# A matrix product on one core: first tiles of x on two DMA queues, and the last 256 columns of w loaded as fp32

## The chip, the cores and the metric

The kernel runs on one core of a Trainium2 chip. The metric is device microseconds of one execution. The core has a matrix engine (TensorE, PE in the profile), two engines that copy, cast and add (VectorE or DVE, ScalarE or ACT), GpSimd (POOL), and SyncE (SP), which here issues DMAs only. ScalarE and GpSimd can issue DMAs too, each on a queue of its own; all queues feed the same 16 DMA engines.

## The reference

```python
def setup_inputs():
    batch, seq, hidden = 16, 512, 768
    return {"x": randn(batch, seq, hidden) as float32,
            "w_qkv": randn(hidden, 3 * hidden) as float32}

def reference(x, w_qkv):
    qkv = np.matmul(x, w_qkv)
    q, k, v = the three blocks of 768 columns of qkv
    return np.stack([q, k, v], axis=0).astype(np.float32)
```

So x is a matrix of 8192 rows and 768 columns, w has 768 rows and 2304 columns, and the three blocks of 768 columns of the product go to three planes of the output.

## The kernel before

**Tiles.** x is worked in 32 pairs of row tiles; a pair `p` holds 256 rows, its row tile `r` 128. The 2304 columns of w are cut into two blocks of 1024 (`q` = 0, 1, each of two slices of `CB` = 512 columns) and the 256 columns between them, the remainder (`REM`, tile `w_rem`). The inner dimension of 768 is six slices `j` of 128; `KH` = 3 of them are a K half `h`. From the third pair on, a pair against a block is not multiplied in eight products of halves but in seven, on sums and differences of quarters of x (`sums_x`, tile `s`) and of w (`sum_w`, tiles `t1` to `t4` and `b22`): `do(u, n)` emits product `n` of a `Quad` `u`, with its evacuation from PSUM. Products 1 and 2 use bf16 copies (`xb` and `b1`), the others 32-bit operands. The remainder is multiplied plainly in bf16.

**The start.** The first two pairs (`ND` = 2) are multiplied plainly in bf16, slice by slice, as w lands. All of this order is written out by hand (`manual_schedule`): every engine runs its instructions in the order in which they are emitted, and waits on semaphores for what they need.

- `load_row` loads a row tile of x as 128 rows of 3 KB, `cast_row` casts it to bf16 (VectorE one half of the columns, ScalarE the other, by `copy_halves`), `turn_row` turns it with six transposes on TensorE (L190) into two PSUM tiles and returns a function that copies them to `xb` (again one half each). All four row tiles go on SyncE's queue, one after the other.
- `touch` are two small DMAs on ScalarE's queue, 128 pieces of 128 bytes each: of w, and of x's third row tile. Nothing reads their result.
- `load_slices` puts the slices of the first 1024 columns of w on SyncE's queue behind x: for the first 512 columns slice 0 in two halves, then slices 1 to 5; then six slices of the second 512.
- `busy(n)` are dummy matmuls of zeros (L458). Between the row tiles' turns stand `busy(8)`, `busy(2)`, `busy(2)`, `busy(1)`.
- `block(0, 0, ...)` multiplies the first two pairs (four row tiles) by the first 512 columns of w (L487), when all four row tiles are turned. For slice 0 it does three row tiles on the first 256 columns, the three on the other 256, and then the fourth; after that four whole matmuls per slice. `cast_j` casts a slice of w for it. `block(0, 1, ...)` follows with the second 512 columns; its last three slices are done row tile by row tile.
- `w_rem` is loaded by two DMAs of GpSimd that cast to bf16 on the way (L450). `hold` keeps GpSimd back until the last slice of the first 512 columns has landed.
- `rems_by_halves` then multiplies the two pairs by the remainder: 24 matmuls of 256 columns (L334), all of K half 0, then all of K half 1.
- Meanwhile VectorE turns the third pair of x (`transpose`, L154), ScalarE rounds its rows to bf16 (`round_row`, L207), VectorE makes `t1` to `t4` (`sum_w`, L120) and the sums of x, and GpSimd casts `b22` (L556). Then `u = quad(2, 0)`, the third pair against the first block, starts with `do(u, 1)` and `do(u, 2)`. VectorE's addition in `do(u, 2)` (L273) comes after `t3` and the sums of x.

A DMA is issued on SyncE only when the DMA eight places before it has landed. PSUM has eight banks, which all products and turns share. The tag `"o"` has five buffers of 8 KB per partition, for the quads' outputs.

After the start, `two`, `group` and `last` run the other pairs in a regular order; the change does not touch them.

Of the kernel before, what the change touches and what calls it, by code (L numbers as in the profile page):

```python
# [10 lines left out]
def kernel(  # L11
# [20 lines left out]
    nc = tc.nc  # L32
    P = 128
    G = 32
    B, T, H = x.shape
    M = B * T
    K = H
    N3 = w_qkv.shape[1]
    KT = K // P
# [72 lines left out]
    def sum_w(q, n):  # L112
        t1, t2, t3, t4 = ts[q]
        o, in0, in1 = {
            1: (t1, stage[q, 0, 1], stage[q, 0, 0]),
            2: (t2, stage[q, 1, 1], t1),
            3: (t3, stage[q, 1, 1], stage[q, 0, 1]),
            4: (t4, stage[q, 1, 0], t2),
        }[n]
        nc.vector.tensor_tensor(o, in0, in1, op=sub)  # L120
# [10 lines left out]
    def load_x_rows(p, parts=range(8)):  # L131
        if p not in xin:
            xin[p] = xin_pool.tile([P, 2 * P // G, KC], fp32, name="xin")
        rows = x_flat[p * 2 * P:(p + 1) * 2 * P, :].rearrange("(g b) k -> b g k", b=G)
        for n in parts:
            r, i = divmod(n, 4)
            gs = slice(r * P // G, (r + 1) * P // G)
            nc.sync.dma_start(
                xin[p][i * G:(i + 1) * G, gs], rows[:, gs, i * KC:(i + 1) * KC]
            )  # L140
# [21 lines left out]

    def load_row(p, r):
        if r == 0:
            xin[p] = xin_pool.tile([P, 2, K], fp32, name="xin")
        row = (2 * p + r) * P
        nc.sync.dma_start(xin[p][:, r], x_flat[row:row + P, :])

    def copy_halves(dst, src):
        nc.vector.tensor_copy(out=dst[0], in_=src[0])
# [4 lines left out]
    def cast_row(p, r):  # L177
        if r == 0:
            xc[p] = s_pool.tile([P, 2, K], bf16, name="xc", tag="s")
        halves = (slice(0, K // 2), slice(K // 2, K))  # L180
        copy_halves([xc[p][:, r, n] for n in halves], [xin[p][:, r, n] for n in halves])

    def turn_row(p, r):
        if r == 0:
            xb[p] = xb_pool.tile([P, KT, 2 * P], bf16, name="xb", tag="xb")
        cols = xc[p][:, r, :].rearrange("m (p j) -> m j p", j=KT)
        ks = (slice(0, KH), slice(KH, KT))
        ps = [ps_pool.tile([P, KH, P], bf16, name="ps") for _ in ks]
        for j in range(KT):
            nc.tensor.transpose(ps[j // KH][:, j % KH, :], cols[:, j, :], eye)  # L190
        return lambda: copy_halves(
            [xb[p][:, n, r * P:(r + 1) * P] for n in ks], [t[:] for t in ps]
        )
# [8 lines left out]
    def round_row(p, r, eng):  # L202
        n = slice(r * P, (r + 1) * P)
        if r == 0:
            xb[p] = xb_pool.tile([P, KT, 2 * P], bf16, name="xb", tag="xb")
        if eng is act:
            eng.activation(xb[p][:, :, n], xf[p][:, :, n], ident)  # L207
        else:
            eng.tensor_copy(out=xb[p][:, :, n], in_=xf[p][:, :, n])
# [46 lines left out]
    def bank():  # L256
        return ps_pool.tile([P, CB], fp32, name="ps")
# [61 lines left out]
    def rem_copied(p, ps, eng=nc.sync):  # L319

        def copied():
            o = or_pool.tile([P, 2, REM], fp32, name="orem")
            act.activation(o[:], ps[:], ident)  # L323
            return lambda: eng.dma_start(rows_of(1, p, R_OFF - H, R_OFF - H + REM), o[:])

        return copied

    def rems_by_halves(pairs):
        banks = [ps_pool.tile([P, 2, REM], fp32, name="ps") for _ in pairs]
        for h in range(2):  # L330
            for p, ps in zip(pairs, banks):
                for r in range(2):
                    for j in range(KH):
                        nc.tensor.matmul(  # L334
                            ps[:, r, :], xb[p][:, h * KH + j, r * P:(r + 1) * P],
                            w_rem[h][:, j, :], start=(h == 0 and r == 0 and j == 0),
                            stop=(h == 1 and j == KH - 1), skip_group_check=True,
                        )
        return [rem_copied(p, ps) for p, ps in zip(pairs, banks)]

    def two(a, b, early, u=None, turns=()):

# [83 lines left out]
    ND = 2  # L426
    zero = xb_pool.tile([P, CB], bf16, name="zero", tag="xb")
    nc.vector.memset(zero[:], 0.0)
    load_row(0, 0)
    touch = m_pool.tile([P, 2, G], fp32, name="touch")  # L430
    nc.scalar.dma_start(touch[:, 0], w_qkv.rearrange("(p j) n -> p j n", j=KT)[:, 0, :G])  # L431
    nc.scalar.dma_start(touch[:, 1], x_flat[2 * P:3 * P, :G])
    nc.scalar.activation(tiny[:], zero[:, :1], ident)
    make_identity(nc, eye)
    load_row(0, 1)
    load_row(1, 0)
    load_row(1, 1)
    half = CB // 2
    load_slices(0, [(0, 1, 0, half), (0, 1, half, CB)] + [(j, 1, 0, CB) for j in range(1, KT)])
    load_slices(1, [(j, 1, 0, CB) for j in range(KT)])  # L440
    load_x_rows(2)

    def hold(src):
        mark = m_pool.tile([P, 1], fp32, name="mark")
        nc.gpsimd.tensor_copy(out=mark[:], in_=src)

    hold(stage[0, 1, 0][:, KH - 1, :1])
    for h in range(2):
        rows = w_qkv.rearrange("(p j) n -> p j n", j=KT)[:, h * KH:(h + 1) * KH]
        nc.gpsimd.dma_start(w_rem[h][:], rows[:, :, R_OFF:R_OFF + REM])  # L450
    hold(xin[2][:, 0, :1])
    load_blocks(1, 0)

    def busy(n):

        ps = bank()
        for _ in range(n):
            nc.tensor.matmul(ps[:], zero[:, :P], zero[:], start=True, stop=True)  # L458

    def cast_j(q, c, w, j, eng=act, n=slice(0, CB)):  # L460
        src = stage[q, j // KH, c][:, j % KH, n]
        if eng is act:
            eng.activation(w[:, j, n], src, ident)  # L463
        else:
            eng.tensor_copy(out=w[:, j, n], in_=src)
# [59 lines left out]

    busy(8)
    cast_row(0, 0)
    turned = [turn_row(0, 0)]
    busy(2)
    turned[0]()  # L530
    cast_row(0, 1)
    turned.append(turn_row(0, 1))
    busy(2)
    cast_row(1, 0)
    turned[1]()
    turned.append(turn_row(1, 0))
    busy(1)
    cast_row(1, 1)
    turned[2]()
    cast_j(0, 0, b1[0], 0, dve, lo)  # L540
    turned.append(turn_row(1, 1))
    cast_j(0, 0, b1[0], 0, dve, hi)
    turned[3]()
    for j in range(1, KT):
        cast_j(0, 0, b1[0], j, dve)
    late0 = block(0, 0, b1[0], first)
    for j in range(KH):
        cast_j(0, 1, bt, j, dve)
    for f in late0:
# [3 lines left out]
    cast_j(0, 1, bt, 4, act)  # L553
    cast_j(0, 1, bt, 5, act)
    sum_w(0, 2)
    nc.gpsimd.tensor_copy(out=b22[0][:], in_=stage[0, 1, 1])  # L556
    late = block(
        0, 1, bt, [((j, ), range(4)) for j in range(KH)] + [(range(KH, KT), range(4))]
    )
    rems = rems_by_halves(range(2))  # L560
    transpose(2, 2)

    late[0]()
    late[1]()
    round_row(2, 0, act)
    rem_stores = [rems[0]()]
    late[2]()
    late[3]()
    round_row(2, 1, act)
    rem_stores.append(rems[1]())  # L570
    load_blocks(1, 1)
    for store in rem_stores:
        store()
    load_x_rows(3)
    for p in range(2):
        store_quad(quads[p, 0])
# [2 lines left out]
    sums[0](nc.gpsimd)  # L579
    sums[1](dve)  # L580
    sums[2](dve)
    sum_w(0, 3)
    sums[3](dve)
    sums[4](dve)

    u = quad(2, 0)
    do(u, 1)
    do(u, 2)
    cast_j(1, 0, b1[1], 0)
    rem2 = rem(2)  # L590
    middle(u, (5, 6))
# [120 lines left out]
```

## Time and profile before

| | |
|---|---|
| median of 3 runs | 359.97 us (359.88 to 360.47) |
| the profiled execution | 360.26 us, its span 358.5 us |
| TensorE busy | 351.8 us, 98% of the span |
| VectorE, ScalarE, GpSimd busy | 65%, 52%, 50% |
| HBM read and written | 32.28 MB and 75.50 MB, 301 GB/s over the span |

The page lists for each engine how long it was busy. The chain of waits follows the work that ended last back to the start, at each step to what released it. The timeline lists instructions in order of time with the idle time before them and what ended it. Where the duration of matmuls is given for a group, the matmuls overlap: their starts stand closer than one lasts. In the windows each engine's busy time in a stretch is followed by the granted clock, the busy share of the DMA engines and the GB/s they moved.

### The profile page before, as it was taken

To read this page: it belongs to the slowest core of one execution; us is meant where nothing else is said; L and a number is where in the kernel's file an instruction comes from. 1 tells how busy PE (TensorE), PEld (TensorE's weight loads), DVE (VectorE), ACT (ScalarE), POOL (GpSimd) and SP (SyncE) were. 2 spreads that over 40 slices of the span, in tenths; PEclk is the share of its full clock that TensorE was granted. 3 is DMA by queue.
4 is the path that set the end of the run, shared out by engine and by line. 5 is a ranking of instruction groups with operands and counts; after the bars stand their busy time and mean duration, and the time that the engine had idled before them with its cause. 6 is when DMAs were issued, how large, how long until landed. Compare 5 with 4: busy or idle time off the path is not lost.

```text
span 358.5 us, 5212 instructions
## 1 busy us (share of the span) xinstructions
PE 351.8 (98%) x1760; PEld 252.6 (70%) x1780; DVE 231.7 (65%) x245; ACT 185.5 (52%) x316; POOL 178.5 (50%) x187
## 2 busy tenths in 40 slices
PE   8999999999999999999999999999999999999995
PEld 4465577767768687786867768687776867768764
DVE  3789776878475675746676474676647577544643
ACT  5469644445545545454554545545454544545443
POOL 0223775582664717447372664717447371754420
PEclk9999999999999999999999999999999999999999
DMA  7998999999999898989989799898989989755767
GB/s 265 347 373 313 323 353 360 369 346 342 339 298 317 286 261 328 261 317 299 289 323 250 309 283 332 282 264 329 268 293 307 294 321 251 312 217 224 273 243 256
DMA packets 82106, 107.73 MB, mean 301 GB/s; under 512 B 5408, under 2 KB 62240, under 8 KB 82080
## 3 DMA queue, kind: packets, MB, share of 16 engines
q1 hardware_dynamic: 74288, 101.86, 86.1%
q10 hardware_dynamic: 6992, 5.15, 5.9%
q0 software_dynamic: 800, 0.39, 0.8%
q8 instruction: 14, 0.23, 0.3%
q14 instruction: 12, 0.10, 0.1%
HBM read 32.28 MB, written 75.50 MB: 301 GB/s over the span
## 4 chain that ended last, share of the span: by engine, by line
PE 93%; DMA 4%; ACT 1%; ACTq 1%; issue 0%
PE ps L251 78%; PE ps L306 11%; PE ps L487 4%; DMA st<-in_w_qkv_dram 3%; DMA touch<-in_x_dram 1%; PE ps L334 1%; ACT o L286 0%; ACTq L385 0%; ACT orem L399 0%; ACT both L463 0%; ACTq L431 0%; ACTq L401 0%; ACTq L399 0%
## 5 line engine op out<-in xcount | busy, mean ns | idle before, releaser
L251 PE MATMUL ps<-t,s 128*128 128x512 f32 x720 | 178.5, 396 | 0.0
L251 PEld LDWEIGHTS ps<-t,s 128*128 128x128 f32 x720 | 134.9, 188 | 29.8 <-ACT o L276 0.3
L154 DVE STREAM_TRANSPOSE xf<-xin 128x1536 f32<-128x1536 f32 (+1 forms) x33 | 91.2, 2767 | 2.5 <-DMA xin<-in_x_dram 2.5
L218 POOL TENSOR_TENSOR s<-xf 128x384 fp32r<-128x384 f32 x29 | 30.8, 1061 | 116.4 <-PE ps L251 115.0
L251 PE MATMUL ps<-b,xb 128*128 128x512 bf16 x342 | 81.7, 379 | 1.2
L283 DVE TENSOR_TENSOR o<-o,ps 128x512 f32<-128x512 f32 x58 | 39.7, 685 | 60.2 <-ACT o L282 60.2
L251 PEld LDWEIGHTS <-xb 128*128 128x128 bf16 x360 | 33.8, 98 | 36.9 <-issue 4.7
L273 DVE TENSOR_TENSOR o<-o,ps 128x512 f32<-128x512 f32 x60 | 39.0, 681 | 29.5 <-PE ps L251 22.4
L282 ACT ACTIVATE o<-ps 128x512 f32<-128x512 f32 x58 | 34.7, 598 | 44.2 <-PE ps L251 44.2
L276 ACT ACTIVATE o<-ps 128x512 f32<-128x512 f32 x60 | 36.0, 600 | 36.6 <-PE ps L251 34.0
L289 DVE TENSOR_TENSOR o<-o,ps 128x512 f32<-128x512 f32 x60 | 41.1, 687 | 20.7 <-PE ps L251 19.6
L260 ACT ACTIVATE o<-ps 128x512 f32<-128x512 f32 x60 | 35.7, 597 | 31.3 <-PE ps L251 18.3
L251 PE MATMUL ps<-b,s 128*128 128x512 f32 x180 | 50.4, 389 | 0.0
L198 POOL CAST xb<-xf 128x1536 bf16<-128x1536 f32 x28 | 41.0, 1464 | 16.7 <-DVE xf L154 16.7
L286 ACT ACTIVATE o<-ps 128x512 f32<-128x512 f32 x60 | 35.9, 598 | 24.3 <-PE ps L251 21.3
L306 PE MATMUL ps<-w_rem,xb 128*128 128x256 bf16 x360 | 44.6, 273 | 0.0
L306 PEld LDWEIGHTS <-xb 128*128 128x128 bf16 x360 | 34.9, 98 | 11.0 <-issue 1.1
L251 PEld LDWEIGHTS ps<-b,s 128*128 128x128 f32 x180 | 33.8, 188 | 7.1
L219 POOL TENSOR_TENSOR s<-s,xf 128x384 fp32r<-128x384 f32 x29 | 29.3, 1009 | 1.3
L220 POOL TENSOR_TENSOR s<-xf 128x384 fp32r<-128x384 f32 x29 | 29.3, 1009 | 0.0
L222 POOL TENSOR_TENSOR s<-xf,s 128x384 fp32r<-128x384 f32 x29 | 29.3, 1009 | 0.0
L323 ACT ACTIVATE orem<-ps 128x512 f32<-128x512 f32 x31 | 18.5, 597 | 20.7 <-PE ps L306 10.9
(47 smaller groups left out, 127.4 us busy)
## 6 DMA issues: line engine op xcount, KB each, us to landing
out_dram<-o SPq DMA_DIRECT2D x62, 768.0 KB, 4.5
xin<-in_x_dram SPq DMA_DIRECT2D x90, 192.0 KB, 6.5
out_dram<-o SPq DMA_DIRECT2D x65, 256.0 KB, 3.7
out_dram<-orem SPq DMA_DIRECT2D x31, 256.0 KB, 5.5
xin<-in_x_dram ACTq DMA_DIRECT2D x22, 192.0 KB, 6.9
st<-in_w_qkv_dram SPq DMA_DIRECT2D x11, 256.0 KB, 5.2
st<-in_w_qkv_dram SPq DMA_DIRECT2D x3, 768.0 KB, 10.0
xin<-in_x_dram SPq DMA_DIRECT2D x4, 384.0 KB, 4.5
```

The lines of the kernel that those rows point to most:

```text
L154: lambda g=g: nc.vector.transpose(turned[:, g:g + n], rows[:, g:g + n])
L198: nc.gpsimd.tensor_copy(out=xb[p][:], in_=t[:])
L218: 1: lambda g: g.tensor_tensor(s[:, 1], a21, a22, op=add),
L251: nc.tensor.matmul(ps[:], lhs[j], rhs[j], start=(start and j == 0), stop=(j == KH - 1), skip_group_check=True,)
L260: nc.scalar.activation(u.o[:, 0, :CB], u.x[:], ident)
L273: nc.vector.tensor_tensor(c11, c11, u.z[:], op=add)
L276: nc.scalar.activation(c12, u.x[:], ident)
L282: nc.scalar.activation(c22, u.x[:], ident)
L283: nc.vector.tensor_tensor(c22, c22, u.y[:], op=add)
L286: nc.scalar.activation(c21, u.x[:], ident)
L289: nc.vector.tensor_tensor(c12, c12, u.y[:], op=add)
L306: nc.tensor.matmul(ps, xb[p][:, j, r * P:(r + 1) * P], w_rem[j // KH][:, j % KH, :], start=(j == 0), stop=(j == KT - 1), skip_group_check= ...
```

## The change

The second row pair goes on ScalarE's queue, beside the first on SyncE's, and the `touch` of x is dropped. VectorE casts 448 of the 768 columns of a row tile instead of 384, and copies four of the six turned slices instead of three. The first three row tiles are turned, and their first 256 columns multiplied, before the fourth row tile is turned (`turn_last`, called inside `block`); slice 0's second 256 columns are cast by ScalarE. The remainder's columns of w come as fp32 by SyncE's queue in two K halves, each in front of one half of the third pair's load; GpSimd casts them to bf16, ahead of `b22`. They use a buffer of the tag `"o"`. `hold` and GpSimd's DMAs are gone. Products 1 and 2 of `u` stand between the two K halves of the remainder's products (`rems_half`), the remainders are evacuated behind `u`'s product 1 and the rounding of the third pair's second row tile, and VectorE's addition of product 2 comes ahead of `t3`.

```diff
-    def load_row(p, r):
+    def load_row(p, r, eng=nc.sync):
...
-        nc.sync.dma_start(xin[p][:, r], x_flat[row:row + P, :])
+        eng.dma_start(xin[p][:, r], x_flat[row:row + P, :])
...
     def cast_row(p, r):
...
-        halves = (slice(0, K // 2), slice(K // 2, K))
+        halves = (slice(0, K * 7 // 12), slice(K * 7 // 12, K))
...
     def turn_row(p, r):
...
-        ks = (slice(0, KH), slice(KH, KT))
-        ps = [ps_pool.tile([P, KH, P], bf16, name="ps") for _ in ks]
-        for j in range(KT):
-            nc.tensor.transpose(ps[j // KH][:, j % KH, :], cols[:, j, :], eye)
+        ks = (slice(0, KT - 2), slice(KT - 2, KT))
+        ps = [ps_pool.tile([P, n.stop - n.start, P], bf16, name="ps") for n in ks]
+        for n, t in zip(ks, ps):
+            for j in range(n.start, n.stop):
+                nc.tensor.transpose(t[:, j - n.start, :], cols[:, j, :], eye)
...
-    def rems_by_halves(pairs):
-        banks = [ps_pool.tile([P, 2, REM], fp32, name="ps") for _ in pairs]
-        for h in range(2):
...
-        return [rem_copied(p, ps) for p, ps in zip(pairs, banks)]
+    def rems_half(pairs, banks, h):
+        for p, ps in zip(pairs, banks):
+            for r in range(2):
+                for j in range(KH):
+                    nc.tensor.matmul(
+                        ps[:, r, :], xb[p][:, h * KH + j, r * P:(r + 1) * P],
+                        w_rem[h][:, j, :], start=(h == 0 and r == 0 and j == 0),
+                        stop=(h == 1 and j == KH - 1), skip_group_check=True,
+                    )
...
-    load_row(0, 0)
-    touch = m_pool.tile([P, 2, G], fp32, name="touch")
-    nc.scalar.dma_start(touch[:, 0], w_qkv.rearrange("(p j) n -> p j n", j=KT)[:, 0, :G])
-    nc.scalar.dma_start(touch[:, 1], x_flat[2 * P:3 * P, :G])
+    touch = m_pool.tile([P, G], fp32, name="touch")
+    nc.scalar.dma_start(touch[:], w_qkv.rearrange("(p j) n -> p j n", j=KT)[:, 0, :G])
+    for r in range(2):
+        load_row(0, r)
+        load_row(1, r, nc.scalar)
...
-    load_row(0, 1)
-    load_row(1, 0)
-    load_row(1, 1)
...
-    load_x_rows(2)
-
-    def hold(src):
-        mark = m_pool.tile([P, 1], fp32, name="mark")
-        nc.gpsimd.tensor_copy(out=mark[:], in_=src)
-
-    hold(stage[0, 1, 0][:, KH - 1, :1])
-    for h in range(2):
-        rows = w_qkv.rearrange("(p j) n -> p j n", j=KT)[:, h * KH:(h + 1) * KH]
-        nc.gpsimd.dma_start(w_rem[h][:], rows[:, :, R_OFF:R_OFF + REM])
-    hold(xin[2][:, 0, :1])
+    st_rem = o_pool.tile([P, KT, REM], fp32, name="str", tag="o")
+    load_w(st_rem[:, :KH], 0, KH, R_OFF, REM)
+    load_x_rows(2, range(4))
+    load_w(st_rem[:, KH:], KH, KH, R_OFF, REM)
+    load_x_rows(2, range(4, 8))
     load_blocks(1, 0)
...
     busy(8)
     cast_row(0, 0)
-    turned = [turn_row(0, 0)]
-    busy(2)
-    turned[0]()
+    turned = turn_row(0, 0)
+    busy(3)
+    turned()
     cast_row(0, 1)
-    turned.append(turn_row(0, 1))
-    busy(2)
     cast_row(1, 0)
-    turned[1]()
-    turned.append(turn_row(1, 0))
-    busy(1)
+    turned = [turn_row(0, 1), turn_row(1, 0)]
+    busy(3)
+    for f in turned:
+        f()
+    cast_j(0, 0, b1[0], 0, dve, lo)
     cast_row(1, 1)
-    turned[2]()
-    cast_j(0, 0, b1[0], 0, dve, lo)
-    turned.append(turn_row(1, 1))
-    cast_j(0, 0, b1[0], 0, dve, hi)
-    turned[3]()
-    for j in range(1, KT):
-        cast_j(0, 0, b1[0], j, dve)
-    late0 = block(0, 0, b1[0], first)
+    cast_j(0, 0, b1[0], 0, act, hi)
+
+    def turn_last():
+        turn_row(1, 1)()
+        for j in range(1, KT):
+            cast_j(0, 0, b1[0], j, dve)
+
+    late0 = block(0, 0, b1[0], first, {0: turn_last})
...
     sum_w(0, 2)
+    for h in range(2):
+        nc.gpsimd.tensor_copy(out=w_rem[h][:], in_=st_rem[:, h * KH:(h + 1) * KH])
     nc.gpsimd.tensor_copy(out=b22[0][:], in_=stage[0, 1, 1])
...
-    rems = rems_by_halves(range(2))
+    banks = [ps_pool.tile([P, 2, REM], fp32, name="ps") for _ in range(ND)]
+    rems_half(range(ND), banks, 0)
     transpose(2, 2)
 
     late[0]()
     late[1]()
     round_row(2, 0, act)
-    rem_stores = [rems[0]()]
+    u = quad(2, 0)
+    u.x, u.z = bank(), bank()
+    for n, ps in ((1, u.x), (2, u.z)):
+        product(u, n, ps, True)
+    rems_half(range(ND), banks, 1)
     late[2]()
     late[3]()
+    evacuate(u)
     round_row(2, 1, act)
-    rem_stores.append(rems[1]())
     load_blocks(1, 1)
-    for store in rem_stores:
-        store()
+    for p, ps in enumerate(banks):
+        rem_copied(p, ps)()()
     load_x_rows(3)
...
+    c11 = u.o[:, 0, :CB]
+    dve.tensor_tensor(c11, c11, u.z[:], op=add)
     sum_w(0, 3)
...
-    u = quad(2, 0)
-    do(u, 1)
-    do(u, 2)
     cast_j(1, 0, b1[1], 0)
```

More of the change, by code (lines that the diff above doesn't have):

```diff
@@ L326, in rem_copied @@
         return copied
-    def rems_by_halves(pairs):
-        banks = [ps_pool.tile([P, 2, REM], fp32, name="ps") for _ in pairs]
-        for h in range(2):
[L331 to L338, printed above, removed]
-        return [rem_copied(p, ps) for p, ps in zip(pairs, banks)]
+    def rems_half(pairs, banks, h):
[7 more added lines that the diff above has]
+                    )
     def two(a, b, early, u=None, turns=()):
```

## The prediction

> **What bounds the kernel now.** I read the page first: part 1 for the bounding engine, part 4 for the chain.
>
> ```profile
> PE 351.8 (98%) x1760; PEld 252.6 (70%) x1780; DVE 231.7 (65%) x245; ACT 185.5 (52%) x316; POOL 178.5 (50%) x187
> ```
>
> TensorE is busy for 98% of the span, and the change adds no matmul that computes (one dummy L458 more). So only the start can move. Next the chain of waits, in order of time, for the first 24 us:
>
> ```profile
> 1.18 4.04 DMA touch<-in_x_dram
> ...
> 5.23 5.24 DMA st<-in_w_qkv_dram
> ...
> 10.48 6.09 DMA st<-in_w_qkv_dram
> ...
> 16.60 0.64 ACT both L463
> ...
> 17.28 2.32 PE ps L487 x10
> 19.60 2.62 PE ps L334 x24
> ```
>
> Loads set the end up to 16.6 us; from 17.28 on the chain stays on TensorE. After that I find one wait of 0.1 us (near 26.9) and no other. So a shift of the first L334 matmul (it starts at 19.43 in the list of TensorE's instructions) goes into the total one for one, if no new wait comes behind it. Now the timeline between 4 and 10 us (start, duration, engine, line):
>
> ```profile
> 6.49 0.84 PE L190 MATMUL ps<-eye,xc 128*128 128x128 bf16 x6
> ...
> 6.72 0.36 DVE L172 CAST xc<-xin 128x384 bf16<-128x384 f32 x1 [0.89 <-DMA xin<-in_x_dram]
> ...
> 7.05 0.36 DVE L172 COPY xb<-ps 128x384 bf16<-128x384 bf16 x1
> ...
> 7.60 0.50 PE L190 MATMUL ps<-eye,xc 128*128 128x128 bf16 x6
> ...
> 7.88 0.36 DVE L172 CAST xc<-xin 128x384 bf16<-128x384 f32 x1 [0.47 <-DMA xin<-in_x_dram]
> ...
> 8.42 0.49 DVE L465 CAST b<-st 128x256 bf16<-128x256 f32 x2
> ...
> 8.46 0.54 PE L190 MATMUL ps<-eye,xc 128*128 128x128 bf16 x6
> ...
> 9.23 0.43 DVE L465 CAST b<-st 128x512 bf16<-128x512 f32 x1
> ```
>
> Call the four row tiles of x X0, X1 (pair 0), X2, X3 (pair 1). X3 lands last (cast at 7.88), its turns run at 8.46, real matmuls start at 8.83. From there to 19.43 are 10.60 us. Work: 6 half matmuls at 0.109 us and 45 whole ones at 0.216 (12 L487 at 28.41 take 2.76, less 0.38 for the last, over 11) are 10.37. The missing 0.23 is the wait for the cast at 16.60. So before 19.43 TensorE has only two things to win: an earlier start, and those 0.23.
>
> **The loads of x.** What two queues do to each other shows in the issues of the first half microsecond (KB, us to landing):
>
> ```profile
> xin<-in_x_dram SPq DMA_DIRECT2D x1, 384.0 KB, 3.3
> touch<-in_w_qkv_dram ACTq DMA_DIRECT2D x1, 16.0 KB, 3.5
> ```
>
> 16 KB on ScalarE's queue took as long as 384 KB beside it on SyncE's. Both are 128 row pieces: the queues take turns, piece for piece. In the changed kernel ScalarE's queue holds touch, X2, X3 and SyncE's X0, X1, then w. So X0 lands as now (0.74 + 3.3 = 4.05), and X1 and X2 share the next stretch and land together, where X2 lands now: 6.70. X1, which landed by 5.5 (its cast starts then, without a wait), comes later. Less the removed second touch (128 small pieces, at most 0.2) I take 6.5 for both. X3 then shares with w's first half slice: 7.8, and 7.9 for the slice (now 7.86 and 8.18). The bounds for X1 and X2: 5.5 (X1 today) to 7.0 (X2 today and some stalls of its own).
>
> The row leaves open whether two queues fill gaps. [...]
>
> **Casts and turns, from 6.5.** VectorE's pieces grow to 448 columns (0.36 at 384, 0.28 at 256: 0.39) and its PSUM copies to 512 (0.43); successive ones start some 0.08 before the last one's end. ScalarE's cast of 320 columns is 0.46 (0.52 at 384).
> - X1: VectorE 6.54 to 6.93, ScalarE to 7.00; then X2: to 7.24 and 7.35.
> - X1's turns start at 7.04. Now the copy of three starts 0.56 after the turns (6.49 to 7.05); of four 0.6: copy 7.63 to 8.05. Copy of X2 7.97 to 8.40. First half of w's slice 8.31 to 8.60.
> - TensorE starts the three tiles at 8.64, against 8.83. But X3 comes behind: its VectorE cast 8.51 to 8.90, its turns 8.95 (after 0.33 of matmuls), its copy of four 9.39 to 9.82 (0.41 behind its first turn as now at 8.46, and one turn more), then slice 1 of w 9.73 to 10.16. The second slice starts at 10.20; now it starts at 8.83 + 0.65 + 0.22 = 9.70.
>
> So the start is 0.19 earlier and the point where the stream becomes dense 0.5 later: one VectorE now does in a row two long copies, a cast of w, a cast, a copy and a cast of w, which lay between X landings before. ScalarE takes the second half of w's first slice (8.69 to 9.10), in front of three matmuls that wait for the turns anyway; cost nothing.
>
> **From there to the remainder.** 44 matmuls of 0.216 are 9.50: 10.20 + 9.50 = 19.70, and the 0.23 wait must not come back. Windows of 1 us (PE, PEld, DVE, ACT, POOL, clock, DMA share, GB/s):
>
> ```profile
> 5.00:6.00 1.00, 1.00 (x7) 0.44 (x5) 0.62 (x2) 0.47 (x2) 0.00 (x0) 1.00 0.98 304
> 13.00:14.00 1.00, 1.00 (x6) 0.44 (x5) 0.67 (x2) 0.42 (x1) 0.92 (x2) 1.00 1.05 404
> 16.00:17.00 1.00, 1.00 (x6) 0.46 (x5) 0.48 (x2) 0.56 (x2) 0.00 (x0) 1.00 1.30 218
> ```
>
> GpSimd's two casting DMAs (L450) cut 404 GB/s to 218 from 15 to 18 us, just where w's last slice lands (10.48 + 6.1). Without them that slice lands some 0.6 to 1.0 earlier and its cast ends by 16.7, before TensorE asks (about 17.5). Stall gone: 19.70 against 19.43, **+0.27**.
>
> **The remainder.** Two fp32 loads of 384 KB go into SyncE's queue, ahead of each half of x's third pair and of all later loads: 1.0 us each at 400 GB/s, against the DMAs removed. First half lands near 16.7 (slice 5 at 15.7 plus 1.0), second 19.0 to 19.5 behind half of xin. GpSimd's casts are 0.73 each (half of the 1.46 of L198), but:
>
> ```profile
> 18.87 1.47 POOL L556 CAST b<-st 128x1536 fp32r<-128x1536 f32 x1
> ...
> 30.22 3.02 POOL L618 CAST b<-st 128x1536 fp32r<-128x1536 f32 x1 [6.46 <-DMA st<-in_w_qkv_dram]
> ...
> 37.93 2.20 POOL L209 CAST xb<-xf 128x768 bf16<-128x768 f32 x1 [4.69 <-DVE xf L154]
> ```
>
> The same cast takes 1.55 longer while VectorE runs L120 (30.17 to 31.92). So 0.73 to 2.2: first half ready by 18.9, wanted at 19.70; second by 21.4, wanted at 19.70 + 1.31 + 1.29 = 22.3. Cover 0.8 and 0.9; if it is gone, TensorE waits for the rest. b22 waits behind them on GpSimd to about 23, wanted at 27.7: nothing.
>
> The products of pair 2 now stand between the halves, so its first rows are wanted at 21.0, not 22.05. Now they are ready at 20.35 + 0.84 = 21.2. The first xin half lands at 17.9 to 18.6 (1.0 more in front, L450 and the late slice gone; now 18.7), VectorE 1.60, ScalarE 0.84: 20.4 to 21.2. Price 0 to 0.2; I take 0, as the slices before it come earlier. VectorE's add of c11 (0.60) moves ahead of t3 and s3; s3 ends at 26.32 now and is wanted at 26.9, and its transposes start about 0.9 earlier: nothing; without that lead, under 0.1. The fourth bank of block(1, 0) waits for that add (24.2), TensorE comes at 27.
>
> **Sum.** +0.5 at the second slice, -0.23 for the wait, 0 behind: +0.27, bounds -0.05 to +0.7 (X2 landing at 6.0: 0.5 less, of which turns that are still slow before 7.3 give 0.2 back, so -0.05; at 7.0: 0.35 to 0.5 more with slices of w to match, so +0.6; late rows of pair 2 another 0.1). Against the profiled execution, 360.26 us, that is 360.5; its median stands 0.29 lower, so **360.2 us**. A measurement of this kernel tells about 0.2% (0.72 us) from no change, so this is no change. Chance 0.42.
>
> **Rivals.**
> - *Two queues fill gaps* (0.28). For: x moved at 304 to 345 GB/s, w at over 400. If X1 and X2 land by 5.5 to 6.0 and turns run fast, X1's chain starts 0.5 to 1.0 earlier: +0.27 less 0.4 to 1.1, so 359.1 to 359.8. [...] Faster by 0.2% in 0.16.
> - *TensorE stays slow longer* (0.18, slower). The profile's clock reads 1.00, but matmuls start 0.42 apart to 5.7 (8 in 3.59), and turns take 0.84 at 6.49, 0.50 at 7.60: full speed comes at about 7.3, after a stretch with only 0.4 us idle. Now TensorE would idle some 0.5 before X1's turns, with X1 later. If full speed slips to 2 us behind the first real matmul, half of those 2 us is lost, and 0.3 on the turns: with +0.27, 361.3 to 361.9. It decides from an idle gap above 0.4, which still passed. [...]
> - *X2 or the third pair late* (0.12). Without its touch X2 lands after 7.1, or TensorE waits for pair 2 or w_rem: +0.7 to +1.2, 360.7 to 361.2; over 0.2% in 0.10.
>
> **How the numbers follow.** Faster 0.16; same 0.42 + 0.12 + 0.02 = 0.56; slower 0.18 + 0.10 = 0.28. The range takes in forecast, third and most of the first rival and the lower half of the second: 359.2 to 361.5. The likeliest case alone: 359.9 to 360.7.
>
> **What would show it.** Right: X1 and X2 casts near 6.5, first L487 near 8.6, L333 near 19.7, no ScalarE wait before the last ten of block 1, dense behind. Wrong: X1 and X2 casts before 6.0; turns still 0.1 apart after 8; TensorE idle between 19.7 and 23.

## The result, and the profile after

The changed kernel takes 362.22 us, the median of 6 runs (361.98 to 363.17); the kernel before, beside it on the same chip, 360.22 us. The ratio is 1.0062, with a 95% interval of 1.0049 to 1.0075: slower by 2.0 us, where 360.2 and no change had been forecast, and outside the range of 359.2 to 361.5. The profiled execution is the slowest of the six, 363.17 us with a span of 361.0; it is read below against the span of 358.5 before, a difference of 2.5.

Between the two profiled executions (363.17 and 360.26) lie 2.9 us, so 0.4 of them are outside the span, from the first instruction to the last, that the profile shows. They are there in every run: with the changed start for x (its two queues, casts and turns, called the head below) an execution takes 2.1 to 2.2 us more than its span, with the old one 1.7 to 1.8. They come behind the last instruction: in the traces the last semaphore update follows it by 2.26 to 2.29 us with the new head and by 1.90 with the old, and up to 1.68 us the two are alike. What is done there, and why the head makes it longer, stays open.

Part 1 of the page gives TensorE 0.8 us more of busy time, where the span is 2.5 us longer:

```profile
PE 352.6 (98%) x1761; PEld 252.0 (70%) x1781; DVE 230.0 (64%) x244; ACT 185.4 (51%) x317; POOL 177.0 (49%) x185
```

The chain of waits (start, duration, what) no longer stays on TensorE from 17.28:

```profile
1.17 5.37 DMA xin<-in_x_dram
...
6.56 4.08 DMA st<-in_w_qkv_dram
...
10.66 7.08 DMA str<-in_w_qkv_dram
...
17.76 0.31 SPq L138
...
18.11 5.30 DMA xin<-in_x_dram
...
23.53 1.56 DVE xf L154
...
25.11 0.84 ACT xb L208
```

SyncE's queue sets the end up to 23.4: the first half of the remainder's columns (`str`) lands at 17.74, the last piece of the third pair at 23.41 (near 21.0 before). VectorE's transpose and ScalarE's rounding follow. The row at 17.76 is an issue on SyncE: the last two pieces of the pair stand eight places behind `str` and the pair's first piece, and are issued only when these have landed (at 17.76 and 18.11). What that costs by itself no run tests. The timeline shows who asks for them:

```profile
6.40 0.70 DVE L172 CAST xc<-xin 128x448 bf16<-128x448 f32 x2 [0.73 <-DMA xin<-in_x_dram]
...
8.48 0.50 PE L477 MATMUL ps<-b,xb 128*128 128x256 bf16 x3
...
17.79 0.99 POOL L547 CAST w_rem<-str 128x768 bf16<-128x768 f32 x1 [16.50 <-DMA str<-in_w_qkv_dram]
...
19.19 1.55 DVE L154 STREAM_TRANSPOSE xf<-xin 128x768 f32<-128x768 f32 x1 [1.08 <-DMA xin<-in_x_dram]
...
19.62 1.47 PE L333 MATMUL ps<-w_rem,xb 128*128 128x256 bf16 x12
...
21.67 1.47 PE L252 MATMUL ps<-b,xb 128*128 128x512 bf16 x5 [0.58 <-ACT xb L208]
...
23.53 1.55 DVE L154 STREAM_TRANSPOSE xf<-xin 128x768 f32<-128x768 f32 x1 [2.80 <-DMA xin<-in_x_dram]
...
26.01 0.83 PE L307 MATMUL ps<-w_rem,xb 128*128 128x256 bf16 x6 [0.91 <-ACT xb L208]
...
29.40 0.93 PE L252 MATMUL ps<-t,s 128*128 128x512 f32 x3 [0.30 <-ACT o L495]
```

Up to the first remainder matmul all is near the forecast. Behind it are three waits that the kernel before lacks: before product 1, before the third pair's second row tile, and before product 7. The brackets count from a modelled end of the matmuls; by their starts (less 0.109 us for a matmul of 256 columns and 0.216 for one of 512) the waits are 0.74, 1.07 and 0.46. With the 0.19 by which the first remainder matmul is later (19.62 against 19.43) and 0.1 of waits that are gone, they make 2.4 of the 2.5.

Why the loads are late is in the windows (PE, PEld, DVE, ACT, POOL, clock, DMA share, GB/s):

```profile
16.00:17.00 1.00, 1.00 (x6) 0.44 (x5) 1.00 (x3) 1.00 (x3) 0.00 (x0) 1.00 1.12 317
17.00:18.00 1.00, 1.00 (x6) 0.49 (x5) 1.00 (x1) 0.21 (x2) 0.21 (x1) 1.00 1.11 265
...
20.00:21.00 1.00, 1.00 (x10) 0.73 (x8) 0.73 (x1) 0.23 (x1) 0.35 (x1) 1.00 1.00 244
```

The DMA engines are busy all the time (share of 1.00 and more), and move 244 to 265 GB/s where 400 had been assumed. There is no casting DMA of GpSimd left that could be blamed.

### The profile page after: what moved, and what is told of

The parts are those of the page before. It is cut to its first block, busy times and chain, and to the rows that moved or that the text cites. A ratio compares the mean times of both kernels' runs of the same rounds, so it can differ in the third digit from the quotient of the medians.

```text
span 361.0 us, 5209 instructions
## 1 busy us (share of the span) xinstructions
PE 352.6 (98%) x1761; PEld 252.0 (70%) x1781; DVE 230.0 (64%) x244; ACT 185.4 (51%) x317; POOL 177.0 (49%) x185
## 4 chain that ended last, share of the span: by engine, by line
PE 86%; DMA 8%; DVE 2%; ACT 1%; ACTq 1%; issue 1%; SPq 0%; DVEq 0%
PE ps L252 76%; PE ps L307 10%; DMA xin<-in_x_dram 4%; DMA str<-in_w_qkv_dram 2%; DVE xf L154 1%; DMA st<-in_w_qkv_dram 1%; DVE t L120 1%; DMA out_dram<-o 1%; ACT o L287 0%; ACTq L383 0%; ACT orem L324 0%; ACT xb L208 0%; ACT orem L397 0%; ACTq L428 0%; SPq L325 0%
## 5 line engine op out<-in xcount | busy, mean ns | idle before, releaser
L252 PEld LDWEIGHTS ps<-t,s 128*128 128x128 f32 x720 | 134.9, 188 | 30.3 <-ACT o L495 0.8
L261 ACT ACTIVATE o<-ps 128x512 f32<-128x512 f32 x60 | 35.8, 597 | 31.3 <-PE ps L252 18.6
L199 POOL CAST xb<-xf 128x1536 bf16<-128x1536 f32 x28 | 41.0, 1463 | 17.9 <-DVE xf L154 17.9
L252 PEld LDWEIGHTS ps<-b,s 128*128 128x128 f32 x180 | 33.8, 188 | 7.1
```

Of the source, the lines that this page charges most:

```text
L199: nc.gpsimd.tensor_copy(out=xb[p][:], in_=t[:])
L252: nc.tensor.matmul(ps[:], lhs[j], rhs[j], start=(start and j == 0), stop=(j == KH - 1), skip_group_check=True,)
L261: nc.scalar.activation(u.o[:, 0, :CB], u.x[:], ident)
```

## The experiments

Ratios are to the kernel before, run beside it on the same chip. Theory A: the remainder's part of the change costs, by the late third pair. Its rivals, as they came up: B, the head (the first tiles of x on two queues) costs; C, a 16 KB load of instructions that falls between the third pair's last pieces; D, TensorE's new order; E, the third pair's own loads, each to 32 of the 128 partitions, are slow and hold up what stands behind them in the queue.

### The two parts apart

**Head alone**: the changed kernel with the remainder's loads, casts and order as before.

```diff
-    st_rem = o_pool.tile([P, KT, REM], fp32, name="str", tag="o")
-    load_w(st_rem[:, :KH], 0, KH, R_OFF, REM)
-    load_x_rows(2, range(4))
-    load_w(st_rem[:, KH:], KH, KH, R_OFF, REM)
-    load_x_rows(2, range(4, 8))
+    load_x_rows(2)
...
+        nc.gpsimd.dma_start(w_rem[h][:], rows[:, :, R_OFF:R_OFF + REM])
...
-    rems_half(range(ND), banks, 0)
+    rems = rems_by_halves(range(2))
...
+    u = quad(2, 0)
+    do(u, 1)
+    do(u, 2)
```

> The kernel after, with the remainder's part of the change undone (GpSimd's casting DMAs, the old order of loads and products). Theory A, the third pair's load is late because the remainder's fp32 loads stand in front of it: 0 to 0.3 us above the kernel before, the second slice at about 10.1 and the first remainder matmul at 19.6 to 19.7, no wait behind it above 0.3. Rival B, the new head costs the loss (two queues, late second slice): 1.5 to 2.0 above the kernel before.

**Remainder alone**: the kernel before with just these lines changed the other way.

> The kernel before, with only the remainder's part of the change. Theory A: 1.5 to 2.2 us above the kernel before, with waits before product 1 of the third pair (0.7) and before its second row tile's remainder (about 1). Rival B: within 0.3 of the kernel before.

Measured: head alone 360.23 us, ratio 1.0005 (0.9997 to 1.0014); remainder alone 362.11, ratio 1.0051 (1.0038 to 1.0065). In the profile of the head alone the second slice starts at 9.57 and the first remainder matmul at 19.07, both 0.5 to 0.6 earlier than expected, and TensorE's only wait behind 10 us is one of 0.10. Its spans are 0.2 shorter than those of the kernel before (median 358.1 against 358.3), and the 0.4 outside the span take that back. The remainder alone has waits of 1.50 before product 1, 0.51 before the second row tile and 0.45 before product 7. The first two places are the expected ones, with more before product 1 and less before the second row tile; the third is new. B falls as the main cause: the remainder's part brings 1.8 us without the head.

### The order of the loads, of the code and of the products

**The whole pair ahead of the second remainder half.**

```diff
     load_w(st_rem[:, :KH], 0, KH, R_OFF, REM)
-    load_x_rows(2, range(4))
+    load_x_rows(2)
     load_w(st_rem[:, KH:], KH, KH, R_OFF, REM)
-    load_x_rows(2, range(4, 8))
```

> The kernel after, with all eight pieces of the third pair loaded between the remainder's two halves (after: half, four pieces, half, four pieces). Theory A: the pair's last piece lands near 21 instead of 23.4, the wait of 1.07 before its second row tile's remainder goes, the wait of 0.7 before product 1 stays, the second half of the remainder is ready at about 22 and just in time: 0.9 to 1.4 us below the kernel after. Rival B: no change.

Measured: 361.58, ratio 1.0038 (1.0024 to 1.0051). By the ratios that is 0.9 below the changed kernel, at the low end of the expectation, with an interval of about 0.7 to either side. The wait moved to the load that is now last:

```profile
18.68 3.00 DVE L154 STREAM_TRANSPOSE xf<-xin 128x768 f32<-128x768 f32 x2 [1.08 <-DMA xin<-in_x_dram]
...
22.24 0.83 POOL L546 CAST w_rem<-str 128x768 bf16<-128x768 f32 x1 [3.95 <-DMA str<-in_w_qkv_dram]
...
23.12 1.47 PE L333 MATMUL ps<-w_rem,xb 128*128 128x256 bf16 x12 [0.48 <-POOL w_rem L546]
```

The pair has landed by 19.9 and the wait before the second row tile is gone, but `w_rem`'s second half is ready only at 23.1, 0.65 too late, and 0.97 stays before product 1. Neither of the two orders serves all who wait for these loads.

**The instruction load earlier.** TensorE's instructions are themselves loaded (queue q8 in the DMA view); a load of 16 KB took 1.17 us of one DMA engine at 20.37 in the changed kernel. More dummy instructions at the start move it to 15.74.

```diff
-        for _ in range(n):
-            nc.tensor.matmul(ps[:], zero[:, :P], zero[:], start=True, stop=True)
+        for _ in range(n * CB // cols):
+            nc.tensor.matmul(ps[:, :cols], zero[:, :P], zero[:, :cols], start=True, stop=True)
...
-    busy(8)
+    busy(8, P)
```

> The kernel after, with the eight first dummy matmuls of 512 columns made into 32 of 128 columns: the same time on TensorE, 48 instructions more, so that the load of TensorE's next instructions (a 16 KB piece of 1.17 us on one DMA engine, at 20.4 in the kernel after, between the third pair's pieces) comes some us earlier. Theory C, this load holds up the pair's last pieces: they land near 21.5 instead of 23.4, and the time is 0.7 to 1.1 us below the kernel after. Theory A with bytes alone: within 0.3 of the kernel after, the last piece near 23.

Measured: 362.81, ratio 1.0066 (1.0051 to 1.0080). Now the first half of the pair is the later one (landed 20.08 instead of 19.06), and TensorE waits 1.66 before product 1 instead of before the second row tile. The last piece comes at 23.16. So C does not explain the loss by where this load falls: it decides which half is late, not how late the sum is. But the load was moved and not taken out: here `str` lands at 18.79, 1.05 later than in the changed kernel. What the time would be without it stays open.

**The old order on TensorE**: both K halves of the remainder, then products 1 and 2.

```diff
     rems_half(range(ND), banks, 0)
+    rems_half(range(ND), banks, 1)
...
-    rems_half(range(ND), banks, 1)
```

> The kernel after, with TensorE's order of before: both K halves of the remainder, then products 1 and 2 of the third pair. Theory A, the landing of the pair's second half sets the time: a wait of about 0.6 for the second half of w_rem, none or little before product 1, the wait before the pair's second row tile as late as in the kernel after; within 0.3 of the kernel after. Rival D, the new order costs it: 0.7 or more below the kernel after.

Measured: 362.18, ratio 1.0052 (1.0038 to 1.0066). Product 1 does not wait any more, but the second remainder half does (0.55), then the second row tile (0.51) and product 7 (0.44). By the ratios the time is 0.4 below the changed kernel, within the noise, and not the 0.7 or more of D. D falls.

### Without the remainder's loads

```diff
-    st_rem = o_pool.tile([P, KT, REM], fp32, name="str", tag="o")
-    load_w(st_rem[:, :KH], 0, KH, R_OFF, REM)
...
-    load_w(st_rem[:, KH:], KH, KH, R_OFF, REM)
...
-        nc.gpsimd.tensor_copy(out=w_rem[h][:], in_=st_rem[:, h * KH:(h + 1) * KH])
+        nc.gpsimd.tensor_copy(out=w_rem[h][:], in_=stage[0, h, 0][:, :, :REM])
```

> The kernel after, without the remainder's two loads: GpSimd casts columns of w's first slices in their place, so the 256 remainder columns of pairs 0 to 30 and of the last are products with other columns of w. Theory A, the bytes in front of the third pair cost the loss: the pair's first half lands near 17.5 and its last piece near 19.5, no wait before product 1, 0 to 0.3 us above the kernel before. Rival D, the new place of the products in TensorE's order costs it: still 1.0 or more above the kernel before.

Measured: 361.82, ratio 1.0054 (1.0041 to 1.0068): no gain, a miss. The pair had landed by 18.5, but GpSimd, with its input there earlier, cast `b22` beside VectorE's `t2`:

```profile
16.35 1.47 POOL L545 CAST b<-st 128x1536 fp32r<-128x1536 f32 x1 [4.28 <-DMA st<-in_w_qkv_dram]
...
16.37 3.06 DVE L120 TENSOR_TENSOR t<-st,t 128x1536 fp32r<-128x1536 f32 x1 [0.58 <-DMA st<-in_w_qkv_dram]
```

The sum took 3.06 instead of 1.75, the transposes began at 19.35, and product 1 waited 0.92. So the run tested something else. Two more runs of this kernel, without the two loads, hold `b22` back until the pair's first rows are there; the second also takes `w_rem` from slices 3 to 5, since GpSimd's earlier cast had cost VectorE's casts of the first slices 0.4.

```diff
+    mark = m_pool.tile([P, 1], fp32, name="mark")
+    nc.gpsimd.tensor_copy(out=mark[:], in_=xin[2][:, 0, :1])
     nc.gpsimd.tensor_copy(out=b22[0][:], in_=stage[0, 1, 1])
```

> [...] Theory A (the bytes of the two fp32 loads ahead of the pair make it late): the pair's halves land by 17.9 and 18.7, VectorE begins to transpose near 18.2, TensorE waits under 0.2 before product 1 and not at the second row tile, the time is within 0.4 us of the kernel before. If the time stays 1 us or more above it with no wait behind 10 us, the pair's lateness is not the cause and something outside the start is.

> As e9 (no loads of the remainder, b22's cast held until the third pair's first rows have landed), but w_rem is cast from w's slices 3 to 5, after VectorE's casts of the first slices (so the remainder's columns are other numbers). Theory A: no 0.4 at the second slice beyond the changed kernel's own, no wait above 0.2 behind it, time -0.2 to +0.4 against the kernel before. If it stays 0.6 or more above with no wait, the rest of the 2.0 is not the loads'.

Measured: 361.29, ratio 1.0023 (1.0013 to 1.0033), and 361.06, ratio 1.0017 (1.0007 to 1.0028). The waits before the second row tile and before product 7 are gone in both, that before product 1 is 0.15. The first, 0.8 above the kernel before, lies between its two expectations, and has the 0.4 of the first slices in it. In the second, 1.6 of the changed kernel's 2.2 us (by ratios) are gone without the two loads; of the 0.6 that are left, 0.4 are the head's time outside the span. Its profiled execution (362.01) is nearly 1.0 above its median, and has a wait of 0.50 up to 17.64, for a slice of w of the second 512 columns. Its windows show what stands beside that wait:

```profile
15.00:16.00 1.00, 1.00 (x6) 0.47 (x5) 1.00 (x2) 0.86 (x3) 0.00 (x0) 1.00 1.06 190
16.00:17.00 1.00, 1.00 (x7) 0.47 (x5) 0.26 (x1) 0.54 (x2) 0.00 (x0) 1.00 0.89 186
```

With busy DMA engines (1.06) only 190 GB/s are moved, with nothing in flight but slices of w and the third pair. The +0.4 expected of the run at most was passed by 0.2, less than this wait.

### The third pair over all partitions

`load_x_rows` brings a half of the pair in four DMAs, each of 128 rows and 192 columns into one group of 32 partitions. Here each of the eight writes 128 partitions, in as many 768-byte pieces. The edit changes a second thing with it: a DMA now reads its 128 rows in their order, one for each partition, where before each of its 32 partitions got four rows that lie 32 rows apart.

```diff
+            if p == 2:
+                row = (2 * p + r) * P
+                nc.sync.dma_start(
+                    xin[p][:, n], x_flat[row:row + P, i * KC:(i + 1) * KC]
+                )
+                continue
```

In the changed kernel:

> The kernel after, with the third pair's eight DMAs of 96 KB laid over 128 partitions each instead of 32: as many pieces of 768 bytes, as many DMAs, the same rows of x; the pair's columns come to other partitions, so its output is not the product. Theory E, the pair's DMAs are slow because each goes to 32 partitions: the pieces take 36 to 40 ns instead of about 50, 16 to 20 us move 350 GB/s or more instead of about 265, the pair's last piece lands near 20, and the time is 1.3 us or more below the kernel after. If it is only the bytes or the number of DMAs: within 0.4 us of the kernel after.

In the kernel before:

> The kernel before; the third pair's eight DMAs write 128 partitions each (rows of a row tile, a quarter of the columns: the pair's data are in other places, so its output is other numbers). Theory E: 15 to 18 us move over 320 GB/s where the kernel before has 218 to 259, although GpSimd's casting DMAs are there; w's last slice lands before 16.4, the wait of 0.23 near 17 goes, the time is 0 to 0.4 below the kernel before. The prediction's reading (the casting DMAs cut the rate): 215 to 270 GB/s from 15 to 18 us, time as before.

In the kernel before with only the remainder's part:

> The kernel before with only the remainder's part of the change, and the third pair's DMAs over 128 partitions as in the run of the changed kernel that did so (pair's data in other places). If the 0.5 left there was the head's later second slice: no wait behind 10 us above 0.15, time 0.2 to 0.5 below the kernel before. If the remainder's part still costs with fast loads: a wait before product 1 or a remainder half, time 0.3 to 0.8 above it.

Measured, as differences to the kernel before worked out from the ratios (us, at 360 us), beside the same kernels with the pair as it is:

| remainder, and head | pair to 32 partitions | pair to 128 partitions |
|---|---|---|
| casting DMAs, old head | 0 (the kernel before) | -0.5 (-0.8 to -0.2) |
| fp32 loads, old head | +1.8 (1.4 to 2.3) | 0.0 (-0.4 to +0.4) |
| fp32 loads, new head | +2.2 (1.8 to 2.7), the changed kernel | +0.5 (0.1 to 0.9) |

With the pair over 128 partitions the fp32 loads cost 0.5 (0.0 less -0.5, with about 0.5 to either side); with the pair to 32 partitions 1.8. The +0.5 in the last row is nearly all the head's time outside the span: the spans are as long as before (median 358.55 against 358.5). The windows of the run with neither the casting DMAs nor the slow pair:

```profile
16.00:17.00 1.00, 1.00 (x6) 0.49 (x5) 1.00 (x2) 0.50 (x1) 0.18 (x1) 1.00 1.10 369
17.00:18.00 1.00, 1.00 (x7) 0.44 (x5) 0.98 (x2) 0.66 (x2) 1.00 (x1) 1.00 1.09 383
```

and of the kernel before with a fast pair, where the casting DMAs are the only slow ones left:

```profile
15.00:16.00 1.00, 1.00 (x6) 0.48 (x5) 1.00 (x2) 1.00 (x4) 0.09 (x1) 1.00 1.22 309
16.00:17.00 1.00, 1.00 (x7) 0.41 (x6) 1.00 (x2) 0.62 (x2) 1.00 (x2) 1.00 1.37 223
```

So the two causes are separate: with the third pair alone the rate is 190 (above), with the casting DMAs alone 223, with neither 369 to 383. The expectation for the kernel before, over 320 GB/s throughout, did not hold; w's last slice landed at 15.58 and the wait of 0.23 went, as expected. In the changed kernel with the fast pair the time came as expected (1.7 below by the ratios), and a 768-byte piece took 36 ns (median) where the changed kernel has 46; but the rate was over 350 from 16 to 18 us only (361 and 367, then 327 and 235), and the last piece landed at 21.16, not near 20. With the old head neither expectation came: the difference is 0.0, with one wait, of 0.42 before product 7.

So E holds as the larger share of A, as far as the layout of the pair's DMAs goes: the remainder's loads are late because they share the queue with loads that move at half the rate (190 GB/s against 369 to 383), and the pair is late because 768 KB more stand in its queue. That it is the number of partitions, and not the order in which the rows are read, is not shown: no run changes one without the other at full use of the DMA engines.

**The same with the data in place.** One DMA for each group of 32 rows, its four quarters to the four partition groups, in the kernel before, the changed kernel, and the kernel before with the remainder's part:

```diff
+                nc.sync.dma_start(
+                    xin[p][:, g],
+                    x_flat[(2 * p * P + g * G):(2 * p * P + (g + 1) * G), :].rearrange(
+                        "b (i k) -> i b k", k=KC
+                    ),
+                )
```

> The kernel before; only the third pair's eight DMAs are cut otherwise: each brings 32 rows, with their four quarters of 192 columns to the four groups of 32 partitions, so each writes all 128 partitions (same 768-byte pieces, same number, same place in memory). Theory E (DMAs that go to 32 partitions each move slowly and hold up what shares the DMA engines with them): the 218 to 259 GB/s from 15 to 18 us rise above 320, w's last slice lands before 16.4 (16.57 before), the wait of 0.23 ahead of the last ten matmuls of block 1 goes, the time is 0 to 0.4 us below the kernel before. The prediction's reading (GpSimd's two casting DMAs cut the rate there): the rate stays at 215 to 270 from 15 to 18 us, and the wait stays.

> The changed kernel, with only the third pair's eight DMAs cut to write all 128 partitions each, now with the rows where they belong (the earlier run over 128 partitions had the pair's data in other places). Theory E: as that run, 1.3 to 1.7 us below the changed kernel, 0.2 to 0.7 above the kernel before, over 320 GB/s from 16 to 19 us, first half landed near 18.2, no wait of TensorE behind 10.2 above 0.15. If E's gain came from the other placement of the data: 0 to 0.5 below the changed kernel.

> The kernel before with only the remainder's part of the change, and the third pair's DMAs cut to write all 128 partitions each. Its start is the old one, where the second slice comes 0.4 earlier than in the changed kernel, and the fp32 loads take no casting DMA. Theory E, with the head costing 0.4 at the second slice: no wait behind 9 us above 0.15, first remainder matmul near 19.0, time 0.2 to 0.6 us below the kernel before and below the run of the changed kernel with the same DMAs. If the pair's loads are not all of it: a wait before product 1 stays, and the time is 0.5 to 1.5 above the kernel before.

Measured: 367.92, 366.75 and 366.54 us, ratios 1.0206 (1.0191 to 1.0221), 1.0175 (1.0152 to 1.0199) and 1.0174 (1.0150 to 1.0198). All missed, and say nothing on E. In the third of them the DMA engines are mostly idle while the pair lands:

```profile
20.00:21.00 1.00, 0.84 (x8) 0.49 (x6) 0.00 (x0) 0.00 (x0) 0.00 (x0) 1.00 0.28 96
```

The DMA share is 0.28, about 4 of 16 engines. Why so few are busy no run shows.

**Two partition groups at a time, on two queues**, with the data in place, in the kernel before:

```diff
-            nc.sync.dma_start(
+            eng.dma_start(
...
-    load_x_rows(2)
+    load_x_rows(2, (0, 1, 4, 5))
...
     for h in range(2):
+        load_x_rows(2, (4 * h + 2, 4 * h + 3), nc.gpsimd)
```

> The kernel before, with four of the third pair's eight DMAs (the upper two groups of 32 partitions) issued by GpSimd on its own queue, ahead of the remainder's casting DMAs. If several partition groups at once lift the rate: over 300 GB/s from 15 to 18 us, the pair's first half landed by 17.5 (17.70 for the third quarter, 18.59 for the fourth in the kernel before), time 0 to 0.5 below the kernel before. If the pattern is slow whatever is beside it: 210 to 270 GB/s, the remainder later by 0.5 to 1 and a wait of TensorE before it; time 0.2 to 1 above.

Measured: 370.19, ratio 1.0257 (1.0229 to 1.0285). SyncE's queue, four loads shorter, went on to the next block of w, and GpSimd's loads, the remainder's among them, had to share with it: TensorE waited 4.8 us for `w_rem`. The expectations missed. Whether two groups at once are faster stays open (183 to 275 GB/s from 15 to 18 us, the casting DMA in them). No arrangement tried with the pair's data in place beats the kernel before.

### The addition of product 2

```diff
-    c11 = u.o[:, 0, :CB]
-    dve.tensor_tensor(c11, c11, u.z[:], op=add)
     sum_w(0, 3)
     sums[3](dve)
     sums[4](dve)
+    c11 = u.o[:, 0, :CB]
+    dve.tensor_tensor(c11, c11, u.z[:], op=add)
```

> The changed kernel, with VectorE's addition of product 2 (L500 and after: c11) put back behind t3 and the sums of x, as in the kernel before. If the place of the addition makes the wait before product 7: that wait (0.46) is under 0.1 and the time 0.3 to 0.5 below the changed kernel; the waits of 0.7 and 1.1 before it stay. If the late pair alone makes it: the wait stays at 0.3 or more, time within 0.2 of the changed kernel.

Measured: 362.31, ratio 1.0055 (1.0040 to 1.0070). The wait before product 7 is gone (0.11 is left, as before), so it is made by the place of the addition; the waits of 1.12 before product 1 and 0.42 before the second row tile stay. The gain of 0.3 to 0.5 is not shown: by the ratios the time is 0.25 us lower, with intervals of 0.5 to either side. The wait also came with a fast pair and the old head (0.42), so a late pair is not needed for it.

## Why the prediction was wrong, point by point

**Loads of x.** X1 and X2 were to land together near 6.5: VectorE casts them one right behind the other from 6.40. In every profiled execution with this head for which the trace has these landings, the two land within 0.22 us of each other, so the touch row was read rightly (from 3.0 to 3.5 us of the kernel before, 72 pieces of SyncE's queue moved beside 75 of ScalarE's). But when they land differs: at 6.38 and 6.54 here, between 5.66 and 6.64 over ten executions, and in two of the ten both by 6.0, where the rival *two queues fill gaps* had put them. In one of these (the whole pair ahead of the second remainder half) real matmuls started 0.7 us earlier than in the profiled changed kernel:

```profile
7.75 0.50 PE L476 MATMUL ps<-b,xb 128*128 128x256 bf16 x3
```

So the rival did not come in the profiled execution, and is not refuted.

**Start.** First real matmuls 8.64 forecast, 8.48 measured; second slice 10.20 and 10.13; first remainder matmul 19.70 and 19.62, without the wait of 0.23. The sum of +0.27 was met by +0.19. The head alone over many runs is +0.2 (-0.1 to +0.5), and its second slice started at 9.57 in the profile, so landing times move this term by half a us from one execution to the next. That the sum met one execution so closely is in part luck, and the sign of the term is not shown.

**A term that the sum has not.** That a shift of the first remainder matmul "goes into the total one for one" holds inside the span only. The head adds 0.4 us behind the last instruction, which the sum has no term for.

**Second rival**, *TensorE stays slow longer*: it did not occur. The turns are up to 0.107 apart to 7.14 and 0.056 behind 7.2, 1.3 us before the first real matmul at 8.48. TensorE had idled 0.45 by the starts just ahead of them, above the 0.4 that the rival names, and full speed came all the same. The 2 us behind the first real matmul, from which its 361.3 to 361.9 are worked out, no run shows.

**The remainder: the step that failed.** "1.0 us each at 400 GB/s" took the best rate of another stage. The slices of w ahead of it came nearly as forecast (the last at 15.92, forecast 15.7), but the first half took 1.82 behind them and came 1.0 late (near 16.7 forecast, 17.74 measured), GpSimd's cast still in time; the pair's first half, 17.9 to 18.6 by the text, let VectorE begin at 19.19; its last piece, which the text had no time for, came at 23.41. Therefore "price 0 to 0.2; I take 0" measured 0.74, and two waits the sum did not have followed: 1.07 for the second row tile, which was never priced, and 0.46 before product 7. The last was named and put at nothing or "under 0.1", because the transposes were to start earlier; the run with the addition put back shows that its place makes the wait. TensorE idle between 19.7 and 23, which the text had named as a sign of being wrong, came at 20.93 to 21.67. The three together are 2.3 of the 2.5 us inside the span.

**Behind that size stands a cause misread.** The text put the dip to 218 GB/s on GpSimd's two casting DMAs, and removed it with them. Half of that is right, as the pair run over 128 partitions shows (223 with the casting DMAs alone). But the third pair's loads make the same dip by themselves (190), and they stay. The row could not tell the two apart, since both were in flight there; the 404 GB/s of 13 to 14 us in the kernel before, where w alone was being moved, should not have been carried past 15.

**Third rival**, *X2 or the third pair late*: the right mechanism, with 0.12 and +0.7 to +1.2 too little chance and half the size. It took one late wait where three followed.

## What to carry to other kernels

Price a load that goes into a queue at the rate of its neighbours in that stage and of that shape, and not at the best rate seen: beside the third pair's 768 KB the DMA engines moved 186 to 190 GB/s with each DMA into 32 partitions, 361 to 383 with each over 128, and 93 to 96 in groups of 32 rows; then write down the landing time of every load behind it and who waits for that. Where two suspects are in flight in the same window, the window does not tell which one is slow: a two-by-two of runs does. If something is taken out to test a wait, hold the other engines to their old times, or the run measures what they do earlier. And compare the time of an execution with its span: a part of a change can act outside the span (0.4 us here).

## What the runs showed of the hardware

- While the third pair's eight DMAs of 96 KB were moved, the DMA engines moved 186 to 190 GB/s (15 to 17 us, without the remainder's loads) with each DMA into 32 partitions and 361 to 383 (16 to 18 us, with the fp32 loads) with each over 128, with the same 768-byte pieces (the rows also read in another order). The load in the same queue slows down too: a 1024-byte piece of the remainder's load took 66 ns (median, 17 to 18 us) in the changed kernel and 46 with the pair over 128 partitions.
- With the third pair in groups of 32 rows the busy share of the 16 DMA engines was 0.27 to 0.28, about four of them, and 93 to 96 GB/s were moved (20 to 22 us, the kernel before with the remainder's part). Why so few, no run shows.
- After a wait of 3.0 us TensorE ran at half speed. In the run with the remainder's part and the pair in groups of 32 rows (the timeline, then a window with its granted clock of 0.50):

```profile
23.69 2.61 PE L260 MATMUL ps<-b,xb 128*128 128x512 bf16 x6 [2.85 <-ACT xb L216]
```

```profile
24.00:25.00 1.00, 1.00 (x4) 0.42 (x3) 0.00 (x0) 0.61 (x2) 0.42 (x1) 0.50 1.03 378
```

  Six matmuls take 2.61 here and 1.47 elsewhere, and the granted clock is 0.50 from 23.9 to 27.3, for 3.4 us. The length of the wait alone does not decide. Counted from the starts, as the 3.0 is, waits of 2.5 us (kernel before with the pair in groups of 32 rows) and 2.65 (changed kernel with these groups) had no such effect, nor had the shorter ones above. But in the latter a second wait of 2.4, 3.3 us behind the end of the 2.65, had it, with a clock of 0.50 from 30.3 to 33.8:

```profile
29.95 1.13 PE L316 MATMUL ps<-w_rem,xb 128*128 128x256 bf16 x6 [2.20 <-ACT xb L217]
```
